# An encoder block with expert retrieval: three quarters of the expert input stage first, selection and gates spread and queued behind weight splits, output groups on two sets of PSUM banks

## The chip, the core and the metric

The kernel runs on one core of one Trainium2 chip. The metric is the device time of one execution in microseconds (us). The engines are PE (TensorE, matmuls), DVE (VectorE), ACT (ScalarE), POOL (GpSimd) and SP (SyncE, which here only issues DMAs). Each engine executes its own instruction stream in order.

## The reference

The block has 256 tokens of width 2048. Token mixers and a cross-attention come first; the change touches only the last part, the retrieval of single-neuron experts:

```python
def peer_ffn(a, w_pq, sub_keys, expert_u, expert_v):
    q = (t @ w_pq).reshape(T, PEER_HEADS, 2, PEER_HALF)
    s = jnp.einsum('thpd,pnd->thpn', q, sub_keys)
    top_s, top_i = lax.top_k(s, PEER_TOPK)                 # 16 of 128 keys, twice per head
    cand = top_s[:, :, 0, :, None] + top_s[:, :, 1, None, :]
    best_s, best_c = lax.top_k(cand.reshape(T, PEER_HEADS, 256), PEER_TOPK)
    i1 = take_along_axis(top_i[:, :, 0], best_c // 16); i2 = take_along_axis(top_i[:, :, 1], best_c % 16)
    expert = i1 * PEER_KEYS + i2                            # one of 16384
    gate = jax.nn.softmax(best_s, axis=-1)
    pre = jnp.einsum('bd,bed->be', t, expert_u[expert])
    act = jax.nn.gelu(pre, approximate=False) * gate
    return jnp.einsum('be,bed->bd', act, expert_v[expert])
```

## The kernel before

For 224 of the 256 tokens (T) the kernel computes all 16384 experts densely and lets a gate that is zero for the unchosen ones do the selecting. For the other 32 tokens it fetches only the chosen rows of `peer_u` and `peer_v` (the sparse part). All matrices are float32; a weight tile is split into a high part `wh` and a rest `wl`, which the PE multiplies one after the other.

**Weight tiles.** The dense part streams 256 tiles of 128x2048 floats (1 MB each). `wtile` (L89 to L101) loads one into a `w` buffer (three, issued by SP), lets ACT cast it to `wh` (L96) and DVE subtract `wl` (L98). With `pool=512` DVE takes 1536 columns and POOL the other 512 (both L101). There are two `wh` and two `wl` buffers. `last_split[0]` remembers the latest DVE split, and `tc.issue_after(last_split[0])` puts an instruction behind it in DVE's order.

**Input stage**, `u_steps(q)`, q = 0 to 3, 32 tiles each: 16 pairs of matmuls (L840 with `wh`, L841 with `wl`), then ACT copy, DVE add and ACT gelu into `P{j//16}` (L843 to L845). Each P tile holds 16 tiles' results, an eighth of the experts. There is not room for all eight, so P0 and P1 are written to DRAM (`pd`) and read back later. In the first quarter (q = 0) POOL helps with the split.

**Selection**, `key_steps` (the key scores' rest, `side`) and `select_steps(1)`, `select_steps(0)`: top 16 of the candidates, softmax, and one-hot products (L725, L731, L732) that look up the indices, all on DVE, 40 steps spread over the first 31 tiles. Nothing ties them to the splits.

**Gates**, `gate_steps`: 28 groups of 8 tokens. DVE makes one-hot matrices (L866 twice, L868 twice: a set), PE multiplies them (L883, 16 small matmuls), ACT copies the result (L893), and POOL writes it to DRAM (`gd`, L898). They are spread over 25 tiles of `u_steps(1)`.

**Preparation**, `prep_steps(c)`: loads the gates of P tile c in two halves (b = 0, 1; L923, by SP, each into one of the three `w` buffers), multiplies eight rows of P by each half (L919, eight DVE instructions), and splits the product into `a` (L107 on ACT, L108 on DVE).

**Output stage**, `v_steps(q)`, 32 tiles each, two chunks c per call in the order of the list `order` (n counts the chunks): per chunk four groups `ds` of four tiles (e = 0 to 3). A group accumulates 4 outputs (f) in four PSUM banks, all from the pool `acc` of four banks (L965 with `wh`, L969 with `wl`). DVE adds them to `yT` in two instructions for each f (L975, L976), and the next group's first matmul into a bank waits for its L976.

**Sparse part**, `sparse_steps`: 32 gathers of `peer_u` rows, each followed by one DVE product and sum (L794), and 32 of `peer_v`, each by a DVE multiply-add (L810). POOL issues each gather (L769) into one of three row buffers. It is spread over 174 tiles from the first preparation on. At its end it is folded in by matmuls (L821, L822).

The tiles are executed in this order: u0 (with selection), u1 (with gates), preparation of c = 2, v0, u2 (with the preparation of c = 4 in its last 7 tiles), v1, u3 (preparation of c = 6 in its last 7), v2, v3.

Of the kernel before, what the change touches and what calls it, by code (L numbers as in the profile page):

```python
# [9 lines left out]
F32 = mybir.dt.float32  # L10
# [4 lines left out]
ALU = mybir.AluOpType  # L15
AX = mybir.AxisListType

P = 128
# [9 lines left out]
TB = 8  # L28
SP = 32
T = S - SP  # L30
# [4 lines left out]
def block_kernel(ctx: ExitStack, tc: tile.TileContext, a: dict, out: bass.AP):  # L35
    nc = tc.nc

    const = ctx.enter_context(tc.tile_pool(name="const", bufs=1))
    stream = ctx.enter_context(tc.tile_pool(name="stream", bufs=2))
# [5 lines left out]
    dram = ctx.enter_context(tc.tile_pool(name="dram", bufs=1, space=bass.MemoryType.DRAM))  # L45
# [8 lines left out]
    def acc(name):  # L54
        return ps_acc.tile([P, 512], F32, tag="acc", name=name)
# [27 lines left out]
    n_w = [0]  # L83
    last_split = [None]

    def wtile(src, pool=0, parts=1):
        n_w[0] += 1
        w = stream.tile([P, D], F32, tag="w", name=f"w{n_w[0]}", bufs=3)
        nc.sync.dma_start(w, src)  # L89
        wh = stream.tile([P, D], F32R, tag="wh", name=f"wh{n_w[0]}")  # L90
        wl = stream.tile([P, D], F32R, tag="wl", name=f"wl{n_w[0]}")
        n = D // parts
        for i in range(parts):
            c = slice(i * n, (i + 1) * n)
            with tc.issue_after(after[-1]) if parts == 4 else nullcontext():
                nc.scalar.copy(wh[:, c], w[:, c])  # L96
            if not pool:
                last_split[0] = nc.vector.tensor_tensor(wl[:, c], w[:, c], wh[:, c].bitcast(F32), op=ALU.subtract).ins  # L98
        if pool:
            for e, c in ((nc.vector, slice(0, D - pool)), (nc.gpsimd, slice(D - pool, D))):  # L100
                i = e.tensor_tensor(wl[:, c], w[:, c], wh[:, c].bitcast(F32), op=ALU.subtract).ins  # L101
                if e is nc.vector:
                    last_split[0] = i
        return wh, wl
# [244 lines left out]
    side = ()  # L349
# [217 lines left out]
    side = ()  # L567
# [194 lines left out]
    act = small.tile([P, SP], F32, tag="act", name="act", bufs=1)  # L762
    hx = None

    bufs = []

    def rows_of(src, k):
        g = bufs[k % 3]
        nc.gpsimd.indirect_dma_start(  # L769
            g, None, src, bass.IndirectOffsetOnAxis(sx[:, 0, k : k + 1].bitcast(U32), 0)  # L770
        )
        return g

    def sparse_input():

        two = [X([P, 2, D], F32, f"rows{i}") for i in range(2)]
        bufs.extend((two[0][:, 1], two[1][:, 0], two[1][:, 1]))
        xs, gb = two[0][:, 0], bufs[2]
        rs = small.tile([P, 1], F32, tag="rs", name="rs", bufs=1)
        bcast_rows(gb, a["g_ffn"])  # L780
        for g in range(NG):
            p = slice(g * SP, (g + 1) * SP)
            nc.gpsimd.dma_start(xs[p], hd[T:S])
            nc.gpsimd.dma_start(rs[p], rf_[P - SP : P, 1:2])
        yield
        with tc.issue_after(last_split[0]):
            nc.vector.scalar_tensor_tensor(xs, xs, rs, gb, op0=ALU.mult, op1=ALU.mult)
        yield xs
# [33 lines left out]
            nc.vector.tensor_tensor(hx[:, 1, fs], hx[:, 1, fs], ps, op=ALU.add)  # L822
        yield

    pd = dram.tile([2, P, 16, T], F32, tag="pd", name="pd")


    ptiles = {}
# [1 line left out]
    def u_steps(q):  # L830

        for j in range(32 * q, 32 * q + 32):
            if j % 16 == 0:
                ptiles[j // 16] = X([P, 16, T], F32, f"P{j // 16}")
            po = acc(f"u{j}")
            wh, wl = wtile(a["peer_uT"][j], 512 if q == 0 else 0)
            wh = wh.rearrange("p (k i) -> p k i", k=NK)
            wl = wl.rearrange("p (k i) -> p k i", k=NK)
            for k in range(NK):
                nc.tensor.matmul(po[:, 0 : 2 * T], wh[:, k, :], aT.both(k), start=(k == 0), stop=False)  # L840
                nc.tensor.matmul(po[:, 0:T], wl[:, k, :], aT.tiles[k // 8][:, k % 8, 0], start=False, stop=(k == NK - 1))  # L841
            pre = ptiles[j // 16][:, j % 16, :]
            nc.scalar.copy(pre, po[:, T : 2 * T])  # L843
            nc.vector.tensor_tensor(pre, po[:, 0:T], pre, op=ALU.add)  # L844
            nc.scalar.activation(pre, pre, AF.Gelu)  # L845
            if j % 16 == 15 and j < 32:
                nc.gpsimd.dma_start(pd[j // 16], ptiles.pop(j // 16))
            yield

# [57 lines left out]
    def prep_steps(c):  # L907

        if c not in ptiles:
            ptiles[c] = X([P, 16, T], F32, f"P{c}b")  # L910
            nc.gpsimd.dma_start(ptiles[c], pd[c])
        pt = ptiles[c]
        g = []
        for b in range(3):
            if b > 0:
                with tc.issue_after(last_split[0]):
                    for j in range(8):
                        pv = pt[:, 8 * b - 8 + j, :].rearrange("p (b t) -> p b t", t=16)
                        nc.vector.tensor_tensor(pv, pv, g[b - 1][:, :, j, :], op=ALU.mult)  # L919
            if b < 2:  # L920
                n_w[0] += 1
                g.append(stream.tile([P, T // 16, 8, 16], F32, tag="w", name=f"w{n_w[0]}", bufs=3))
                nc.sync.dma_start(g[b], gd[:, 2 * c + b])  # L923
            yield
        for e in range(4):
            for i in range(2):
                ahl = M([P, 2, 2, T], F32R, f"a{c}_{e}{i}")
                j = 4 * e + 2 * i
                split(ahl[:, :, 0, :], ahl[:, :, 1, :], pt[:, j : j + 2, :])
                parts[c, 2 * e + i] = ahl  # L930
            yield
# [2 lines left out]
    yT = None  # L934
    gf = None

    order = [2, 3, 4, 5, 6, 7, 0, 1]

    def v_steps(q):

        nonlocal gf, hx, yT
        for n in range(2 * q, 2 * q + 2):
# [7 lines left out]
            if n == 7:  # L950
                gf = X([P, D], F32, "gf")
                bcast_rows(gf, a["g_final"])
            nxt = prep_steps(order[n + 1]) if n in (0, 2, 4, 5, 6) else iter(())
            for ds in range(4):
                po = [acc(f"v{c}_{ds}_{f}") for f in range(4)]
                for e in range(4):
                    wh, wl = wtile(a["peer_vP"][((2 * c + e // 2) * 4 + ds) * 2 + e % 2])
                    wh = wh.rearrange("p (j f) -> p j f", j=4)
# [35 lines left out]
    def run_spread(main, n_main, side, n_side):  # L994

        done = 0
        for i, _ in enumerate(main):
            due = n_side if i >= n_main - 1 else (i + 1) * n_side // n_main
            while done < due:
                next(side, None)  # L1000
                done += 1

    def with_last(main, n, side):

        for i, _ in enumerate(main):
            if i >= 32 - n:
                next(side, None)
            yield

    run_spread(u_steps(0), 31, chain(side, select_steps(1), select_steps(0)), 4 + 18 + 18)  # L1010
    sp = sparse_input()
    next(sp)
    run_spread(u_steps(1), 25, gate_steps(), T // TB + 1)
    xs = next(sp)
    rest = chain(
        prep_steps(2),
        v_steps(0),
        with_last(u_steps(2), 7, prep_steps(4)),
        v_steps(1),
        with_last(u_steps(3), 7, prep_steps(6)),  # L1020
        v_steps(2),
        v_steps(3),
    )
    run_spread(rest, 174, sparse_steps(xs), 2 * SP + 1)


    r = rstd_of(ssq_f, "final")
# [65 lines left out]
```

## Time and profile before

| | us |
|---|---|
| time, median of 3 runs (lowest, highest) | 2614.22 (2614.06, 2616.01) |
| the profiled execution: its own time | 2612.45 |
| the profiled execution: its span | 2610.7 |
| in it, PE busy | 2463.8 |
| in it, DVE busy | 1680.0 |
| in it, ACT busy | 1159.7 |

Busy times of matmuls include their modelled ends, so a busy PE can still be slower than at full clock. The granted clock of a stretch is its mean, 1.00 being 2.4 GHz. The two lists that matter for the dense part are a table of busy times by stretch (its first tile starts at 1096.46 us, its last ends at 2598.60) and the list of what PE waited for.

### The profile page before, as it was taken

The numbers are of one execution on the slowest core, as the hardware profiler recorded it, in microseconds if no ns is written. First come the engines' busy times: TensorE is split into PE (matmuls) and PEld (weight loads), VectorE is DVE, ScalarE is ACT, GpSimd is POOL, SyncE is SP. The second block draws the span as 40 slices with busy tenths as digits, with TensorE's granted clock in tenths as the row PEclk, the third lists the DMA queues.
The fourth block names the chain that finished last, engine by engine and source line by source line (L and its number), as shares of the span: only waits on it lengthen the run. The fifth ranks groups of instructions, "written<-read, shape, count | busy, mean of one in ns | idle before, by whom it ended". The sixth has DMA issues, their size and how long they took to land. (4 is left out here: it accounts for less than half of the span.)

```text
span 2610.7 us, 34575 instructions
## 1 busy us (share of the span) xinstructions
PE 2463.8 (94%) x14266; PEld 2214.9 (85%) x14266; DVE 1680.0 (64%) x2121; ACT 1159.7 (44%) x1346; POOL 236.7 (9%) x184
## 2 busy tenths in 40 slices
PE   8999999999999999977999988999899999898897
PEld 7888888888888888967988878999888998888897
DVE  5556544456555455897377777766777767677665
ACT  5444444545444445533455544345434455343343
POOL 0000000000000000123611101012000122000000
PEclk9999999999999999988999989999999999999999
DMA  6554555555544555434877777777777778876463
GB/s 250 188 193 175 178 193 193 214 189 175 187 171 164 176 201 186 169 122 149 283 254 241 234 266 284 284 281 289 269 281 274 264 290 311 319 286 243 173 221 132
DMA packets 84798, 584.40 MB, mean 224 GB/s; under 512 B 9793, under 2 KB 9857, under 8 KB 18721
## 3 DMA queue, kind: packets, MB, share of 16 engines
q1 hardware_dynamic: 67904, 480.28, 52.1%
q0 software_dynamic: 16592, 101.88, 10.8%
q8 instruction: 112, 1.84, 0.3%
q14 instruction: 46, 0.37, 0.0%
q10 hardware_dynamic: 144, 0.03, 0.0%
HBM read 559.58 MB, written 22.54 MB: 223 GB/s over the span
## 5 line engine op out<-in xcount | busy, mean ns | idle before, releaser
L98 DVE TENSOR_TENSOR wl<-w,wh 128x2048 fp32r<-128x2048 f32 (+2 forms) x432 | 936.6, 2172 | 759.4 <-ACT wh L96 759.0
L96 ACT CAST wh<-w 128x2048 fp32r<-128x2048 f32 (+2 forms) x464 | 841.8, 1819 | 875.1 <-PE v L965 308.4
L965 PE MATMUL v<-a,wh 128*128 128x448 f32 x2048 | 663.8, 383 | 47.3 <-DVE yT L976 40.7
L840 PE MATMUL u<-a,wh 128*128 128x448 f32 x2048 | 666.3, 383 | 4.8 <-ACT wh L96 4.8
L841 PE MATMUL u<-a,wl 128*128 128x224 f32 x2048 | 552.1, 270 | 39.9 <-DVE wl L101 32.7
L969 PE MATMUL v<-a,wl 128*128 128x224 f32 x2048 | 548.0, 268 | 10.4 <-DVE wl L98 10.4
L965 PEld LDWEIGHTS v<-a,wh 128*128 128x128 f32 x2048 | 392.5, 192 | 85.3 <-ACT wh L96 24.6
L841 PEld LDWEIGHTS u<-a,wl 128*128 128x128 f32 x2048 | 400.8, 196 | 44.9 <-DVE wl L101 36.0
L840 PEld LDWEIGHTS u<-a,wh 128*128 128x128 f32 x2048 | 394.0, 192 | 36.5 <-ACT wh L96 5.6
L969 PEld LDWEIGHTS v<-a,wl 128*128 128x128 f32 x2048 | 399.1, 195 | 12.6 <-DVE wl L98 11.8
L845 ACT ACTIVATE P<-P 128x224 f32<-128x224 f32 x128 | 50.1, 392 | 319.4 <-DVE P L844 319.3
L122 PE MATMUL g<-wh,x 128*128 128x512 f32 x256 | 100.2, 391 | 0.0
L124 PE MATMUL g<-wl,x 128*128 128x512 f32 x256 | 99.6, 389 | 0.0
L123 PE MATMUL g<-wh,x 128*128 128x512 f32 x256 | 99.6, 389 | 0.0
L101 DVE TENSOR_TENSOR wl<-w,wh 128x1536 fp32r<-128x1536 f32 x32 | 57.7, 1802 | 60.6 <-ACT wh L96 60.6
L101 POOL TENSOR_TENSOR wl<-w,wh 128x512 fp32r<-128x512 f32 x32 | 75.9, 2373 | 201.5 <-ACT wh L96 164.2
L144 PE MATMUL qk<-x,wh 128*128 128x512 f32 x256 | 91.8, 403 | 0.2 <-DVE qk L150 0.2
L144 PE MATMUL mq<-hq,wh 128*128 128x512 f32 x256 | 90.8, 398 | 0.0
L144 PE MATMUL pq<-hf,wh 128*128 128x512 f32 x256 | 90.8, 398 | 0.0
L769 POOL DMA_INDIRECT rows<-in_peer_v,sx x32 | 54.6, 1706 | 391.9 <-DVE rows L810 327.3
L144 PE MATMUL mk<-mem,wh 128*128 128x512 f32 x256 | 89.7, 394 | 0.0
L769 POOL DMA_INDIRECT rows<-in_peer_u,sx x32 | 51.6, 1613 | 374.4 <-DVE act L794 347.5
(322 smaller groups left out, 3474.4 us busy)
## 6 DMA issues: line engine op xcount, KB each, us to landing
w<-in_peer_uT SPq DMA_DIRECT2D x128, 1024.0 KB, 4.9
w<-in_peer_vP SPq DMA_DIRECT2D x128, 1024.0 KB, 4.9
w<-in_w_in SPq DMA_DIRECT2D x72, 1024.0 KB, 4.9
w<-in_mem_w_kv SPq DMA_DIRECT2D x32, 1024.0 KB, 4.8
w<-in_w_out SPq DMA_DIRECT2D x16, 1024.0 KB, 4.8
w<-in_mem_w_q SPq DMA_DIRECT2D x16, 1024.0 KB, 4.9
w<-in_mem_w_o SPq DMA_DIRECT2D x16, 1024.0 KB, 4.9
w<-in_peer_w_q SPq DMA_DIRECT2D x16, 1024.0 KB, 4.8
```

The source lines that it names most:

```text
L96: nc.scalar.copy(wh[:, c], w[:, c])
L98: last_split[0] = nc.vector.tensor_tensor(wl[:, c], w[:, c], wh[:, c].bitcast(F32), op=ALU.subtract).ins
L101: i = e.tensor_tensor(wl[:, c], w[:, c], wh[:, c].bitcast(F32), op=ALU.subtract).ins
L122: nc.tensor.matmul(po[b], xh, wh[:, k, :], start=(kk == 0), stop=False)
L123: nc.tensor.matmul(po[b], xl, wh[:, k, :], start=False, stop=False)
L124: nc.tensor.matmul(po[b], xh, wl[:, k, :], start=False, stop=(kk == nkc * 4 - 1))
L144: nc.tensor.matmul(po[f], wh[:, k, fs], xT.both(kk), start=(kk == 0), stop=False)
L769: nc.gpsimd.indirect_dma_start(g, None, src, bass.IndirectOffsetOnAxis(sx[:, 0, k : k + 1].bitcast(U32), 0))
L840: nc.tensor.matmul(po[:, 0 : 2 * T], wh[:, k, :], aT.both(k), start=(k == 0), stop=False)
L841: nc.tensor.matmul(po[:, 0:T], wl[:, k, :], aT.tiles[k // 8][:, k % 8, 0], start=False, stop=(k == NK - 1))
L965: nc.tensor.matmul(po[f][:, 0 : 2 * T], wh[:, j, fs], ahl.rearrange("p e t -> p (e t)"), start=first, stop=False,)
L969: nc.tensor.matmul(po[f][:, 0:T], wl[:, j, fs], ahl[:, 0, :], start=False, stop=last)
```

## The change

The order of the tiles becomes u0, u1, u2, v0, u3, v1, v2, v3. Everything beside the tiles becomes a track with a first tile, a last tile and a number of steps; the tracks wrapped in `paced` issue all their DVE work behind the latest split. Selection has tiles 0 to 46, gates 46 to 84, the sparse part 50 to 238. The second quarter too shares its splits with POOL. Four P tiles instead of two are written to DRAM and read back, and the list `order` begins with the four that stay. The gates of a preparation go, on POOL's queue, into a single buffer of their own, cut out of what was the third row buffer, so that two row buffers are left. In the output stage the groups with odd `ds` (but not in the last chunk) use the four banks of the pools `pst` and `psm`.

```diff
     def rows_of(src, k):
-        g = bufs[k % 3]
+        g = bufs[k % 2]
...
         two = [X([P, 2, D], F32, f"rows{i}") for i in range(2)]
-        bufs.extend((two[0][:, 1], two[1][:, 0], two[1][:, 1]))
-        xs, gb = two[0][:, 0], bufs[2]
+        bufs.extend((two[0][:, 1], two[1][:, 0]))
+        gates.append(two[1][:, 1, 0 : 8 * T].rearrange("p (b j t) -> p b j t", j=8, t=16))
+        xs, gb = two[0][:, 0], bufs[1]
...
-    pd = dram.tile([2, P, 16, T], F32, tag="pd", name="pd")
+    pd = dram.tile([4, P, 16, T], F32, tag="pd", name="pd")
...
-            wh, wl = wtile(a["peer_uT"][j], 512 if q == 0 else 0)
+            wh, wl = wtile(a["peer_uT"][j], 512 if q < 2 else 0)
...
-            if j % 16 == 15 and j < 32:
+            if j % 16 == 15 and j < 64:
                 nc.gpsimd.dma_start(pd[j // 16], ptiles.pop(j // 16))
...
-        g = []
+        g = gates[0]
...
-                        nc.vector.tensor_tensor(pv, pv, g[b - 1][:, :, j, :], op=ALU.mult)
+                        nc.vector.tensor_tensor(pv, pv, g[:, :, j, :], op=ALU.mult)
             if b < 2:
-                n_w[0] += 1
-                g.append(stream.tile([P, T // 16, 8, 16], F32, tag="w", name=f"w{n_w[0]}", bufs=3))
-                nc.sync.dma_start(g[b], gd[:, 2 * c + b])
+                nc.gpsimd.dma_start(g, gd[:, 2 * c + b])
...
-    order = [2, 3, 4, 5, 6, 7, 0, 1]
+    order = [4, 5, 6, 7, 0, 1, 2, 3]
...
-            nxt = prep_steps(order[n + 1]) if n in (0, 2, 4, 5, 6) else iter(())
+            nxt = prep_steps(order[n + 1]) if n in (0, 2, 3, 4, 5, 6) else iter(())
             for ds in range(4):
-                po = [acc(f"v{c}_{ds}_{f}") for f in range(4)]
+                kinds = (pst, pst, psm, psm) if ds % 2 and n < 7 else (acc,) * 4
+                po = [kind(f"v{c}_{ds}_{f}") for f, kind in enumerate(kinds)]
...
-    run_spread(u_steps(0), 31, chain(side, select_steps(1), select_steps(0)), 4 + 18 + 18)
...
-    run_spread(rest, 174, sparse_steps(xs), 2 * SP + 1)
+    def paced(steps):
+
+        while True:
+            with tc.issue_after(last_split[0]):
+                if next(steps, steps) is steps:
+                    return
+            yield
...
+    main = chain(u_steps(0), u_steps(1), u_steps(2), v_steps(0), u_steps(3), v_steps(1), v_steps(2), v_steps(3))
+
+    tracks = [
+        (paced(chain(side, select_steps(1), select_steps(0))), 0, 46, 4 + 18 + 18),
+        (input_steps(), 28, 46, 3),
+        (paced(gate_steps()), 46, 84, T // TB + 1),
+        (sparse_all(), 50, 238, 2 * SP + 1),
+        (prep_steps(order[0]), 88, 96, 7),
+        (prep_steps(order[2]), 152, 160, 7),
+    ]
+    done = [0] * len(tracks)
+    for i, _ in enumerate(main):
+        for n, (steps, lo, hi, of) in enumerate(tracks):
+            due = 0 if i < lo else min(of, (i + 1 - lo) * of // (hi - lo))
+            while done[n] < due:
+                next(steps, None)
+                done[n] += 1
```

The two kernels have the same matmuls in another order. Three places show what moves.

DVE in the selection, before: between the splits of two successive tiles (`wl193`, `wl194`) stands the add of the input stage (`P0`) and then sixteen instructions of the selection (`oh`, `sel`, `ex`, `cand`).

```order
L101 TENSOR_TENSOR wl193_8461<-w193_8458,wh193_8460 128x1536
L844 TENSOR_TENSOR P0_8017<-u6_8354,P0_8017 128x224
L732 TENSOR_REDUCE sel1_8248<-oh110_8753 128x32
L732 TENSOR_REDUCE sel1_8248<-oh111_8800 128x32
L725 TENSOR_TENSOR oh112_8848<-sel1_8248,iota_90 128x512
L725 TENSOR_TENSOR oh113_8896<-sel1_8248,iota_90 128x512
L731 TENSOR_TENSOR oh112_8848<-oh112_8848,top_7076 128x512
L731 TENSOR_TENSOR oh113_8896<-oh113_8896,top_7076 128x512
L732 TENSOR_REDUCE sel1_8248<-oh112_8848 128x32
L732 TENSOR_REDUCE sel1_8248<-oh113_8896 128x32
L737 SCALAR_TENSOR_TENSOR ex_8943<-sel1_8248 128x128
L689 TENSOR_TENSOR cand00_8960<-top_7076 128x512
```

DVE at the same kind of work in the changed kernel, some tiles later:

```order
L101 TENSOR_TENSOR wl201_8829<-w201_8826,wh201_8828 128x1536
L845 TENSOR_TENSOR P0_8017<-u14_8727,P0_8017 128x224
L725 TENSOR_TENSOR oh100_8868<-sel1_8334,iota_90 128x512
L731 TENSOR_TENSOR oh100_8868<-oh100_8868,top_7076 128x512
L732 TENSOR_REDUCE sel1_8334<-oh100_8868 128x32
L101 TENSOR_TENSOR wl202_8876<-w202_8873,wh202_8875 128x1536
L845 TENSOR_TENSOR P0_8017<-u15_8780,P0_8017 128x224
L725 TENSOR_TENSOR oh101_8915<-sel1_8334,iota_90 128x512
L731 TENSOR_TENSOR oh101_8915<-oh101_8915,top_7076 128x512
L732 TENSOR_REDUCE sel1_8334<-oh101_8915 128x32
L101 TENSOR_TENSOR wl203_8923<-w203_8920,wh203_8922 128x1536
```

The selection's instructions now stand three at a time between two splits.

POOL in the gates, before: after the spill of P1 it issues only the writes of gates, two for each pair of groups.

```order
L847 DMA pd_8014<-P1_8852 128x3584
L898 DMA gd_8015<-gs0_0_9764 128x8x128
L898 DMA gd_8015<-gs0_1_9765 128x8x128
L898 DMA gd_8015<-gs16_0_9908 128x8x128
L898 DMA gd_8015<-gs16_1_9909 128x8x128
```

POOL in the gates of the changed kernel (`rows0`, `rows1` are the sparse part's buffers):

```order
L899 DMA gd_8015<-gs0_0_10414 128x8x128
L899 DMA gd_8015<-gs0_1_10415 128x8x128
L101 TENSOR_TENSOR wl237_10637<-w237_10634,wh237_10636 128x512
L769 DMA rows0_9693<-in_peer_u,sx_8012 128x2048
L101 TENSOR_TENSOR wl238_10712<-w238_10709,wh238_10711 128x512
L101 TENSOR_TENSOR wl239_10785<-w239_10782,wh239_10784 128x512
L899 DMA gd_8015<-gs16_0_10603 128x8x128
L899 DMA gd_8015<-gs16_1_10604 128x8x128
L101 TENSOR_TENSOR wl240_10828<-w240_10825,wh240_10827 128x512
```

A quarter of each tile's split, and gathers, now stand between the writes.

DVE in the gates, before: two sets of one-hot instructions (`oe`, `o2`) stand between two splits, and none of the sparse part.

```order
L844 TENSOR_TENSOR P2_9673<-u47_10790,P2_9673 128x224
L866 TENSOR_TENSOR oe_136_10856<-iotax_92,i1T_7073 128x1024
L866 TENSOR_TENSOR oe_136_10856<-iotax_92,i2T_7074 128x1024
L868 TENSOR_TENSOR o2_136_10857<-oe_136_10856,gT_7075 128x1024 x2
L866 TENSOR_TENSOR oe_144_10929<-iotax_92,i1T_7073 128x1024
L866 TENSOR_TENSOR oe_144_10929<-iotax_92,i2T_7074 128x1024
L868 TENSOR_TENSOR o2_144_10930<-oe_144_10929,gT_7075 128x1024 x2
L98 TENSOR_TENSOR wl235_11011<-w235_11008,wh235_11010 128x2048
```

DVE in the gates of the changed kernel (L795 is L794 of before):

```order
L845 TENSOR_TENSOR P3_10370<-u59_11090,P3_10370 128x224
L867 TENSOR_TENSOR oe_72_11157<-iotax_92,i1T_7073 128x1024
L867 TENSOR_TENSOR oe_72_11157<-iotax_92,i2T_7074 128x1024
L795 ISA rows1_9694,act_8013<-rows1_9694,rows0_9693 128x2048
L795 ISA act_8013 128x1
L869 TENSOR_TENSOR o2_72_11158<-oe_72_11157,gT_7075 128x1024 x2
L867 TENSOR_TENSOR oe_80_11230<-iotax_92,i1T_7073 128x1024
L867 TENSOR_TENSOR oe_80_11230<-iotax_92,i2T_7074 128x1024
L869 TENSOR_TENSOR o2_80_11231<-oe_80_11230,gT_7075 128x1024 x2
L101 TENSOR_TENSOR wl247_11315<-w247_11312,wh247_11314 128x1536
```

A product of the sparse part has come in among the two sets.

## Rows read from the trace of the kernel before

**Rows 1.** Page part 1: busy time, share of the span, instructions of each engine.

```profile
PE 2463.8 (94%) x14266; PEld 2214.9 (85%) x14266; DVE 1680.0 (64%) x2121; ACT 1159.7 (44%) x1346; POOL 236.7 (9%) x184
```

**Rows 2.** Table by stretch: us, busy time (instructions) per engine, PE clock, DMA, GB/s.

```profile
1123.55:1216.84 93.29, 60.83 (x291) 54.72 (x289) 88.89 (x223) 27.96 (x34) 16.85 (x13) 0.82 0.29 103
...
1315.39:1489.01 173.62, 158.85 (x1250) 146.19 (x1249) 131.16 (x158) 95.02 (x188) 24.52 (x29) 0.99 0.76 247
...
1514.08:1538.07 23.99, 12.60 (x66) 11.19 (x65) 22.68 (x35) 9.19 (x15) 4.68 (x4) 0.72 0.90 335
1538.07:1704.50 166.43, 157.83 (x994) 148.28 (x993) 118.47 (x121) 67.77 (x57) 12.24 (x11) 1.00 0.78 279
...
1836.10:1875.82 39.72, 33.98 (x195) 31.24 (x193) 30.51 (x42) 19.49 (x27) 3.98 (x2) 0.91 0.76 272
1875.82:2054.39 178.57, 166.75 (x1026) 156.63 (x1025) 127.58 (x135) 65.77 (x45) 13.08 (x12) 0.97 0.76 272
2054.39:2184.81 130.42, 130.42 (x833) 124.49 (x833) 91.84 (x69) 65.21 (x76) 27.80 (x10) 1.00 0.76 281
2184.81:2220.82 36.01, 32.48 (x194) 30.12 (x193) 28.90 (x38) 19.23 (x27) 7.63 (x6) 0.95 0.94 356
2220.82:2510.05 289.23, 258.38 (x1547) 240.52 (x1545) 200.11 (x229) 104.57 (x75) 13.53 (x13) 0.95 0.70 253
...
sum 1502.14, PE 1377.45 PEld 1289.17 DVE 1066.84 ACT 646.41 POOL 212.63; mean PE 98.39 PEld 92.08 DVE 76.20 ACT 46.17 POOL 15.19
```

**Rows 3.** What PE waited for, 1090 to 2611: us in total, times, longest.

```profile
PE v L965 <- DVE yT L976: 40.7, 18, 6.2
PE u L841 <- DVE wl L101: 32.7, 11, 5.7
PE ps_g L883 <- DVE o L868: 14.7, 24, 2.7
```

**Rows 4.** Groups of instructions, 1315.39 to 1489.01: busy us, mean ns, idle before.

```profile
L98 DVE TENSOR_TENSOR wl<-w,wh 128x2048 fp32r<-128x2048 f32 x25 | 57.2, 2289 | 39.0 <-ACT wh L96 39.0
...
L868 DVE TENSOR_TENSOR o<-oe,gT 128x1024 f16<-128x1024 f16 x54 | 35.0, 689 | 1.0
...
L883 PE MATMUL ps_g<-o,oe 128*128 128x128 f16 x448 | 32.9, 219 | 14.8 <-DVE o L868 14.7
```

**Rows 5.** Groups of DVE, 1090 to 2611: the sparse products.

```profile
L794 DVE CUSTOM_DVE_ANT_0 rows<-rows,rows 128x2048 f32<-128x2048 f32 x21 | 48.0, 2283 | 0.0
```

**Rows 6.** Timelines in the selection (start us, us): POOL and DVE splits of two tiles.

```profile
1167.02 3.28 DVE L101 TENSOR_TENSOR wl<-w,wh 128x1536 fp32r<-128x1536 f32 x1
1167.40 1.27 POOL L101 TENSOR_TENSOR wl<-w,wh 128x512 fp32r<-128x512 f32 x1
...
1218.92 1.76 DVE L101 TENSOR_TENSOR wl<-w,wh 128x1536 fp32r<-128x1536 f32 x1 [4.03 <-ACT wh L96]
1218.97 2.86 POOL L101 TENSOR_TENSOR wl<-w,wh 128x512 fp32r<-128x512 f32 x1 [3.23 <-ACT wh L96]
```

**Rows 7.** Timelines at one end of an output group: DVE, then PE.

```profile
2388.91 0.38 DVE L975 TENSOR_TENSOR yT<-v,yT 128x224 f32<-128x224 f32 x1
2389.21 2.34 DVE L810 SCALAR_TENSOR_TENSOR rows<-rows,act,rows 128x2048 f32<-128x2048 f32 x1
...
2393.68 2.28 DVE L98 TENSOR_TENSOR wl<-w,wh 128x2048 fp32r<-128x2048 f32 x1
...
2392.00 0.71 PE L965 MATMUL v<-a,wh 128*128 128x448 f32 x1 [2.16 <-DVE yT L976]
```

**Rows 8.** Timelines around one gate load: SP, DVE, ACT.

```profile
2255.29 0.33 SPq L923 DMA_DIRECT2D w<-gd  x1
...
2260.20 2.50 DVE L919 TENSOR_TENSOR P<-P,w 128x224 f32<-128x224 f32 x8
...
2266.96 1.90 ACT L96 CAST wh<-w 128x2048 fp32r<-128x2048 f32 x1 [9.00 <-DMA w<-in_peer_vP]
```

**Rows 9.** DMA issues: count, median us to landing.

```profile
rows<-in_peer_u,sx POOLq DMA_INDIRECT x32, 6.1
```

More of the change, by code (lines that the diff above doesn't have):

```diff
@@ L763, in block_kernel @@
     hx = None
-    bufs = []
+    bufs, gates = [], []
     def rows_of(src, k):
-        g = bufs[k % 3]
+        g = bufs[k % 2]
         nc.gpsimd.indirect_dma_start(
@@ L1001, in run_spread, with sparse_all, input_steps @@
                 done += 1
[L1003 to L1007, printed above, removed]
-            yield
-    run_spread(u_steps(0), 31, chain(side, select_steps(1), select_steps(0)), 4 + 18 + 18)
[L1011 to L1023, printed above, removed]
-    run_spread(rest, 174, sparse_steps(xs), 2 * SP + 1)
+    def paced(steps):
[3 more added lines that the diff above has]
+                    return
+            yield
+    xs = []
+    def sparse_all():
+        yield from sparse_steps(xs[0])
+    def input_steps():
+        for x in sparse_input():
+            xs.append(x)
+            yield
+        xs.pop(0)
+    main = chain(u_steps(0), u_steps(1), u_steps(2), v_steps(0), u_steps(3), v_steps(1), v_steps(2), v_steps(3))
[14 more added lines that the diff above has]
+                done[n] += 1
     r = rstd_of(ssq_f, "final")
```

## The prediction

> **What bounds the kernel now.** I read the shares of the engines first: PE is busy for 94% of the span, DVE for 64% [rows 1]. So the PE is the bound, and only what lets it wait or slows its clock can be won. Which stretches those are, the table by stretch tells. An undisturbed stretch, the 26 plain tiles of u3, takes 130.42 us, or 5.016 us a tile, at clock 1.00 [rows 2]. The 256 tiles together take 1502.1 us [rows 2], while 256 times 5.016 is 1284.1: 218.0 us lie above the pace. By stretch, each as its time less its tiles at 5.016 [rows 2]: selection (9 tiles) 48.1; gates (25) 48.2; preparation of c = 2 (2) 14.0; the first output stretch (31) 10.9; u2's tail with a preparation (6) 9.6; the second output stretch (32) 18.1; u3's tail (6) 5.9; the third output stretch (48) 48.5. What is left of 218.0, some 14.7, lies in stretches of a few us each and in the last chunk.
>
> What the PE waits for there comes from the list of its waits [rows 3]: the adds into `yT` in the output stage (40.7 us in 18 waits), the splits with POOL in the selection (32.7 in 11), the one-hot matrices in the gates (14.7 in 24). All three are DVE. So DVE is idle a third of the time and late where its work stands in a lump.
>
> **Selection.** Before, up to sixteen small instructions stand between two splits; in that stretch DVE is busy for 88.89 of 93.29 us and the clock falls to 0.82 [rows 2]. The change removes no instruction; it puts the steps behind splits, 40 over 46 tiles. A tile then asks DVE for a split of 1.76 us [rows 6], an add of 0.4, and three one-hot instructions of some 0.7 each [the like of rows 4, 689 ns]: about 4.3 us of 5.016. That fits; one lump of small instructions at the join of the parts still makes a split late by some 2 us. I take 4 us for what remains of 48.1, with 2 and 12 as ends. Gain 44.
>
> **Gates.** They keep their work and get new neighbours. The 28 groups' matmuls are real PE work: 448 of them [rows 4], about 1.0 us a group where PE waits for nothing, so 28 us. The rest of the 48.2 is waiting and clock, 20. After the change, 38 tiles carry the 28 sets, which alone would thin out the waits; but the sparse part starts at tile 50 now, so that some 12 of its products (65 steps over 188 tiles, 34 tiles of them here) of 2.28 us [rows 5] fall into this stretch, some among two sets between two splits. Two sets are about 8 x 0.69 = 5.5 us; with a product 7.8, more than a tile's 5.016 plus its group. I count ten ordinary waits for one-hots of 1.0, three with a product inside of 3.1, two late splits of together 3.8, and 3 for clock: 26. To this comes POOL's quarter of the split, which this stretch did not have. In the selection a POOL split takes 1.27 us alone, but 2.86 when DVE's split began just ahead of it, and DVE's takes 3.28 instead of 1.76 when POOL's falls into it [rows 6]: one waits out the other. One-hot instructions and products read two inputs as the split does. I put 8 us on this: some 14 of the 38 tiles meet, with 0.6 on the path each, the rest covered by the tile of cushion in the two `wl` buffers. Sum 28 + 26 + 8 = 62. The ends: 48 (28, the 14.7 of [rows 3] and 5) and 75 (28, 14.7, all twelve products at 2.3, and 5). Loss 14. POOL's queue has the writes of gates and the gathers ahead of its splits now; the writes wait for ACT's copies of the gates, but the cast that the split needs stands behind those copies on ACT anyway, so I put nothing on it.
>
> What these rows show has a rule in the Trainium skill, "SBUF — State Buffer", section "Who interferes with whom": a DVE instruction with two SBUF inputs contends with a GpSimd instruction that reads SBUF, and the second to issue is blocked until the first ends. The trace agrees: 3.28 is 1.76 and rather more than the 1.27. The rule speaks against this edit. By it, with every one of the 38 POOL splits shutting DVE out for 1.27 us on the path, the stretch would cost 48 more instead of 8; this is the rival B below, worked out there from the rows.
>
> **Preparations.** The three that stand beside input tiles or alone cost 14.0 + 9.6 + 5.9 = 29.5. Two remain, each in the last eight tiles of an input quarter. Each has two lots of eight multiplies, 2.5 us [rows 8], splits of 0.6 each, and now a sparse instruction. With one gate buffer the second load starts only when the first multiplies are done and lands, by the like of a gather, 6.1 us later [rows 9], so that DVE can stand before it. I take 9.5 each, the dearer of the two tails, 19 together; ends 13 and 26. Gain 10.5.
>
> **Output stage.** Outside the last chunk it holds 10.9 + 18.1 + 48.5 = 77.5. Of this 40.7 are waits for `yT` [rows 3]. They go, as the next group's first matmuls get other banks. What is late next? At the end of a group a sparse multiply-add of 2.34 us slips between the adds, and the split behind them starts at 2393.68 instead of some 2391.4 [rows 7]. Before, the PE waited 2.16 us for the bank and this late split was hidden behind that wait, then the tile ran at a lower clock (0.71 us for a matmul in [rows 7]). After, the PE goes on at once: from 2389.8 one tile of 5.016 lasts to 2394.8, while the split ends at 2396.0. It waits 1.2 to 1.5 us instead of some 4 (an estimate: 2.16, and about a third of a tile lost at the lower clock). I count nine such, 13 us. Second, a gate load sat in one of three `w` slots until its multiplies were done, and the cast after it waited 9.00 us for its weights [rows 8]; with a buffer of its own this goes. What remains besides: the joins of input and output quarters and lots of multiplies, some 7; the fold of the sparse part, about 10, unchanged; two more spills and reads of P and the like, 6. Together 36; ends 22 and 60. Gain 41.
>
> **Two row buffers** instead of three: a gather is issued when the product before last is done, and has 2 x 2.9 tiles, some 14 us from one step to the next, against 6.1 for its landing [rows 9]. Nothing. The last chunk keeps its banks; with the 14.7 of the small stretches it stays.
>
> **Sum.** Selection 4, gates 62, preparations 19, output 36, rest 14.7: 135.7 for 218.0, a gain of 82. The profiled execution took 2612.45, so 2530; the median of the runs lies 1.8 above it: **2532 us**.
>
> **The rivals.** *A, the banks only change the name of the wait:* the splits are as late as the banks were. For it: the sparse instruction in [rows 7] delays both. Against: the split stands a tile ahead. Then 31 of the 40.7 stay: 2563. That the change doesn't do what it says would look like this.
> *B, POOL and DVE lock in the gates:* for it [rows 6]; against, the selection's plain tiles ran at the pace with POOL's 2.86. If each of 38 tiles pays 0.8 to 1.27 on the path, 30 to 48 instead of 8, the time is 2554 to 2572.
> *C, the stalls get so short that the clock holds:* the stretches with clock under 0.96 [rows 2] are those with stalls of several us. With every term at its lower end (2 + 48 + 13 + 22 + 14.7 = 99.7) the gain is 118: 2496.
> *D, slower than before:* the gathers, gate loads, spills and reads of P and writes of gates share POOL's queue, and with two row buffers one late transfer holds the next. The products stand in DVE's order between splits, so a late gather stops the splits behind it. Over 65 steps it takes 82 / 65 = 1.3 us each to eat the gain, that is, landings of about 15.5 us instead of 6.1 [rows 9]. At 2.0 us each it gives 2614 + 130 - 82 = 2662. Against it: 14 us of slack at every step.
>
> **How the numbers follow.** Forecast 0.62, C 0.14, A 0.12, B 0.08, D 0.04. The range leaves out half of C, D, and the upper edges of A and B: 2495 to 2574. A measurement of this kernel can tell about 0.2%, 5 us, from no change. All cases but D are faster by far more: 0.95, allowing a little for D at small size; within 0.2% 0.01; slower 0.04.
>
> **What would show it.** Right: in the selection no wait for a split over 3 us, and the clock near 1.00; no wait of L965 for `yT` outside the last chunk, and short ones (1 to 2 us) for `wl` in their place; no cast waiting 9 us for weights; the gates' 38 tiles at 239 to 266 us (190.6 for the tiles, and 48 to 75), with waits for one-hots. Wrong: waits for splits in the output stage adding up to over 30 us (A); POOL or DVE splits in the gates of 3 us at most tiles with PE behind them (B); DVE waiting for `rows` (D).

## The result, and the profile after

The changed kernel takes 2538.9 us (median of 4 runs, 2532.45 to 2540.6) where the kernel before takes 2614.14 (2611.39 to 2616.01): a ratio of 0.971, 95% interval 0.969 to 0.973. The forecast was 2532, its range 2495 to 2574. The profiled execution took 2540.41 us, its span is 2538.4.

Page part 1 of the changed kernel, to be read beside [rows 1]: PE is busy for 15.8 us less, DVE for 26 us and POOL for 74 us more.

```profile
PE 2448.0 (96%) x14266; PEld 2203.0 (87%) x14266; DVE 1706.1 (67%) x2121; ACT 1158.3 (46%) x1346; POOL 310.9 (12%) x236
```

The table by stretch of the changed kernel (us, busy time of PE, PEld, DVE, ACT, POOL with instructions, PE clock, DMA share, GB/s), to be read beside [rows 2]. The stretches are: selection (tiles 5 to 47), gates (48 to 84), u2's tail with the first preparation and the two tiles behind it (90 to 97), the rest of v0 (98 to 127), u3 (128 to 153), its tail and one tile (154 to 160), v1 to the fold (161 to 238), the fold (239, 240), the rest (241 to 255).

```profile
1125.84:1356.75 230.91, 222.60 (x1385) 209.36 (x1383) 199.06 (x329) 112.81 (x135) 103.86 (x56) 0.99 0.67 230
1356.75:1610.16 253.41, 225.39 (x1635) 209.10 (x1633) 193.85 (x207) 124.64 (x224) 84.93 (x57) 0.97 0.79 276
1635.22:1691.83 56.61, 47.52 (x259) 43.72 (x257) 36.14 (x46) 24.08 (x32) 4.28 (x5) 0.88 0.70 243
1691.83:1844.33 152.50, 151.03 (x963) 143.56 (x961) 113.20 (x117) 66.08 (x55) 12.49 (x12) 1.00 0.80 286
1844.33:1977.02 132.69, 130.89 (x834) 124.42 (x833) 88.30 (x75) 64.83 (x77) 18.54 (x9) 1.00 0.76 278
1977.02:2023.02 46.00, 39.42 (x227) 36.21 (x225) 33.81 (x41) 22.10 (x30) 7.99 (x8) 0.93 0.85 310
2023.02:2425.08 402.06, 394.19 (x2499) 373.36 (x2497) 329.08 (x372) 167.25 (x115) 39.83 (x37) 1.00 0.84 309
2425.08:2442.75 17.67, 15.33 (x74) 12.07 (x73) 11.96 (x18) 5.40 (x6) 0.00 (x0) 0.90 0.50 173
2442.75:2526.22 83.47, 80.91 (x514) 75.13 (x512) 50.78 (x59) 31.07 (x26) 0.00 (x0) 1.00 0.41 140
```

At 5.016 us a tile these stretches lie above the pace by 15.2, 67.8, 16.5, 2.0, 2.2, 10.9, 10.8, 7.6 and 8.2 us. The first five tiles add 1.9, tiles 85 to 89 nothing: all 256 tiles lie 143 us above the pace, for 218.0 before. 75 us have gone, all from this part of the program. (The execution that was profiled started its first tile 2.4 us later than the one before, so the two profiled executions differ by 72.)

What PE waited for, in the changed kernel from 1090 to 2540 (us, times, longest), beside [rows 3], and the longest of its waits for a split, from the timeline:

```profile
PE ps_g L884 <- DVE o L869: 22.5, 22, 2.9
PE u L842 <- DVE wl L98: 11.8, 9, 1.9
PE u L842 <- DVE wl L101: 10.5, 6, 3.2
PE v L969 <- DVE wl L98: 9.3, 12, 1.0
...
1134.42 0.37 PE L842 MATMUL u<-a,wl 128*128 128x224 f32 x1 [3.19 <-DVE wl L101]
```

The 40.7 us for `yT` are gone, the 32.7 for the selection's splits have become 10.5, and the one-hots have risen from 14.7 to 22.5. The longest wait for a split, 3.19 us, comes in tile 6, where the steps of the key scores meet those of the selection: there some 8 us of small DVE instructions still stand between two splits. In place of the banks stand twelve short waits for a split, 9.3 us. One of them, on DVE and PE, at a group end like that in [rows 7]:

```profile
2325.91 0.39 DVE L975 TENSOR_TENSOR yT<-v,yT 128x224 f32<-128x224 f32 x1
2326.21 2.35 DVE L811 SCALAR_TENSOR_TENSOR rows<-rows,act 128x2048 f32<-128x2048 f32 x1
...
2330.69 2.28 DVE L98 TENSOR_TENSOR wl<-w,wh 128x2048 fp32r<-128x2048 f32 x1
...
2333.03 0.37 PE L969 MATMUL v<-a,wl 128*128 128x224 f32 x1 [0.96 <-DVE wl L98]
2333.23 0.38 PE L965 MATMUL v<-a,wh 128*128 128x448 f32 x1
```

The sparse multiply-add still stands between the adds and the split is still late by its length, but PE waits 0.96 us instead of 2.16. Its next matmul of 448 columns takes 0.38 us, where the one in [rows 7] takes 0.71: the granted clock is 1.00 (2.4 GHz) from 2333 to 2338 us, and was 0.50 (1.2 GHz) from 2392 to 2394 before.

### The profile page after: what moved, and what is told of

The parts are those of the page before. It is cut to its first block, busy times and chain, and to the rows that moved or that the text cites. A ratio compares the mean times of both kernels' runs of the same rounds, so it can differ in the third digit from the quotient of the medians.

```text
span 2538.4 us, 34530 instructions
## 1 busy us (share of the span) xinstructions
PE 2448.0 (96%) x14266; PEld 2203.0 (87%) x14266; DVE 1706.1 (67%) x2121; ACT 1158.3 (46%) x1346; POOL 310.9 (12%) x236
## 5 line engine op out<-in xcount | busy, mean ns | idle before, releaser
L98 DVE TENSOR_TENSOR wl<-w,wh 128x2048 fp32r<-128x2048 f32 (+2 forms) x400 | 863.2, 2163 | 654.5 <-ACT wh L96 654.0
L965 PE MATMUL v<-a,wh 128*128 128x448 f32 x2048 | 648.9, 377 | 3.5 <-DVE P L845 3.5
L842 PE MATMUL u<-a,wl 128*128 128x224 f32 x2048 | 549.8, 269 | 22.5 <-DVE wl L98 11.8
L965 PEld LDWEIGHTS v<-a,wh 128*128 128x128 f32 x2048 | 386.0, 188 | 34.1 <-DVE P L845 4.0
L969 PEld LDWEIGHTS v<-a,wl 128*128 128x128 f32 x2048 | 392.5, 192 | 13.8 <-DVE wl L98 13.1
L101 POOL TENSOR_TENSOR wl<-w,wh 128x512 fp32r<-128x512 f32 x64 | 144.1, 2252 | 259.6 <-ACT wh L96 244.4
L101 DVE TENSOR_TENSOR wl<-w,wh 128x1536 fp32r<-128x1536 f32 x64 | 122.7, 1917 | 59.3 <-ACT wh L96 59.3
L769 POOL DMA_INDIRECT rows<-in_peer_v,sx x32 | 48.5, 1517 | 323.4 <-DVE rows L811 280.3
```

Source lines behind the costliest of these rows:

```text
L769: nc.gpsimd.indirect_dma_start(g, None, src, bass.IndirectOffsetOnAxis(sx[:, 0, k : k + 1].bitcast(U32), 0))
L965: nc.tensor.matmul(po[f][:, 0 : 2 * T], wh[:, j, fs], ahl.rearrange("p e t -> p (e t)"), start=first, stop=False,)
L969: nc.tensor.matmul(po[f][:, 0:T], wl[:, j, fs], ahl[:, 0, :], start=False, stop=last)
```

## The experiments

Each stands beside runs of the kernel before on the same chip. Every kernel but the second is the changed one with edits. The runs of the changed kernel alone spread over 8 us, so two of these kernels that lie 3 or 4 us apart are not told apart by their times.

**One set of banks.**

```diff
-                kinds = (pst, pst, psm, psm) if ds % 2 and n < 7 else (acc,) * 4
+                kinds = (acc,) * 4
```

> The changed kernel with all output groups in the four banks of acc again, all else as changed (2538.9 us). Theory (the banks were the wait, and the late splits behind a sparse instruction cost less than the banks did): the waits of L965 for yT come back, about 2.2 us each at 9 or more group ends, with a slow tile behind, and the short waits for wl (1 us, 9.3 us in all) go; 25 to 45 us more, 2564 to 2584. Rival A (the banks only change the name of the wait): 2531 to 2547.

Measured: 2566.5 us, ratio to before 0.981 (0.979 to 0.983); 28 us more than the changed kernel. The waits for `yT` are back, in 18 places:

```profile
PE v L965 <- DVE yT L976: 24.9, 18, 2.2
```

The time lies in the theory's range, and rival A falls. The 24.9 us are less than the 40.7 of [rows 3], though: the long ones, up to 6.2 us, are missing.

**The kernel before with two sets of banks.** The same line, put into the kernel before.

> The kernel before with one edit: odd output groups outside the last chunk in the banks of pst and psm. Theory: the 40.7 us of waits for yT go, with the clock behind them, and some 13 us of late splits come; the gate loads that hold a weight buffer stay; 25 to 50 us less than before, 2564 to 2589. Rival A: 2605 to 2614. If the waits for weights behind a gate load and the waits for yT are one stall counted twice, the gain is under 25.

Measured: 2594.1 us, ratio 0.992 (0.989 to 0.994); 20 us less, where 25 to 50 were expected. The first line is of the kernel before, the others show what came in place of the waits for `yT`:

```profile
PE v L969 <- DVE wl L98: 10.4, 4, 6.6
...
PE v L970 <- DVE wl L98: 25.5, 17, 6.6
...
PE v L966 <- ACT wh L96: 8.4, 5, 3.0
```

So some 23 of the 40.7 us turned into waits for splits and casts. In the kernel before, some waits that bore the banks' name had a second cause behind them, as the last sentence of the expectation allowed.

**Gate loads in the weight buffers.**

```diff
...
-        g = gates[0]
+        g = []
...
-                nc.gpsimd.dma_start(g, gd[:, 2 * c + b])
+                n_w[0] += 1
+                g.append(stream.tile([P, T // 16, 8, 16], F32, tag="w", name=f"w{n_w[0]}", bufs=3))
+                nc.sync.dma_start(g[b], gd[:, 2 * c + b])
```

> The changed kernel with the gate loads as they were: two loads on SP's queue into the weight buffers, and three row buffers. Theory (a gate load in a weight buffer delays the weights behind it): casts wait for weights again, 4 to 9 us each at most of the six preparations inside the output stage; 10 to 30 us more, 2549 to 2569, less some 4 us in the input tails, where the second load no longer waits for the first multiplies. Rival (the second set of banks hides that delay too): 2531 to 2543.

Measured: 2575.1 us, ratio 0.984 (0.982 to 0.987); 36 us more, above the range. Casts of ACT wait for weights 24 times; the second line is of the changed kernel:

```profile
ACT wh L96 <- DMA w<-in_peer_vP: 102.4, 24, 9.4
...
ACT wh L96 <- DMA w<-in_peer_vP: 9.7, 3, 4.2
```

The stretch from v1 to the fold goes from 10.8 to 52.8 us above the pace, while the two input tails get 9 us shorter. The gate loads are the dearer of the two delays of the output stage. The edit moves their buffer, their queue and the number of row buffers together; that it is the weight buffer is read from the casts' waits for weights, and no run parts the three.

**Neither edit of the output stage.** Both diffs above together.

> The changed kernel with both edits of the output stage undone: all output groups in the four banks of acc, and the gate loads in the weight buffers with three row buffers. Undoing the banks alone cost 28 us, undoing the gate loads alone 36. Theory (the two delays fall on the same group ends, and the PE pays the longer of the two): less than their sum, 2580 to 2594. Rival (they add up): 2598 to 2608.

Measured: 2601.5 us, ratio 0.995 (0.993 to 0.996); 62.6 us more than the changed kernel, where 28 and 36 add up to 64. My theory falls: the two add up. The list of waits, and ACT, DVE and PE at the place of PE's wait of 6.67 us:

```profile
PE v L966 <- DVE yT L977: 49.5, 20, 6.7
...
ACT wh L96 <- DMA w<-in_peer_vP: 80.3, 18, 9.5
...
2257.39 1.90 ACT L96 CAST wh<-w 128x2048 fp32r<-128x2048 f32 x1 [7.62 <-DMA w<-in_peer_vP]
...
2259.33 2.29 DVE L98 TENSOR_TENSOR wl<-w,wh 128x2048 fp32r<-128x2048 f32 x1 [4.81 <-ACT wh L96]
...
2264.63 0.71 PE L966 MATMUL v<-a,wh 128*128 128x448 f32 x1 [6.67 <-DVE yT L977]
```

The waits under the banks' name grow from 24.9 to 49.5 us when the gate loads hold weight buffers. A late cast makes a late split; DVE, in order, then comes late to the adds, and PE's wait is booked on `yT`. Why the banks alone gave 20 us in the kernel before and 26 here (2601.5 to 2575.1) was not pursued.

**The sparse part behind the gates.**

```diff
-        (sparse_all(), 50, 238, 2 * SP + 1),
+        (sparse_all(), 85, 238, 2 * SP + 1),
```

> The changed kernel with the sparse part spread over tiles 85 to 238 instead of 50 to 238, so that no product of it stands among one-hot sets. Theory (the products among the sets are the larger part of the new waits in the gates): the 36 gate tiles lose about 17 of the 67.8 us that they lie above 5.016 us a tile, and the output stage gains 3 to 6 us of late splits; 2522 to 2532. Rival B (POOL's split blocking one-hot instructions is the larger part): the gates lose under 5 us; 2536 to 2545.

Measured: 2517.5 us, ratio 0.963 (0.961 to 0.965); 21 us less than the changed kernel, below the range expected. The gates' stretch, 253.41 us there, is

```profile
1352.90:1581.05 228.15, 216.87 (x1634) 202.17 (x1633) 164.09 (x182) 123.81 (x223) 62.99 (x45) 1.00 0.72 249
```

25 us less, where 17 were expected; rival B falls. In the stretch PE's waits for one-hots go from 22.5 to 10.9 us, those for splits from 5.6 to 0.3, and the clock is back from 0.97 to 1.00, which is worth about 8 us of 253 (an estimate). The output stage pays some 9 of the 25 back, and the first input tail gives 6 more. What the product does among the sets is seen on DVE and POOL in the changed kernel; the last line is of another place:

```profile
1422.07 1.49 DVE L867 TENSOR_TENSOR oe<-iotax,i1T 128x1024 f16<-128x1024 f16 x1
...
1424.08 2.28 DVE L795 CUSTOM_DVE_ANT_0 rows<-rows 128x2048 f32<-128x2048 f32 x1
...
1427.50 2.25 DVE L867 TENSOR_TENSOR oe<-iotax,i1T 128x1024 f16<-128x1024 f16 x1
...
1431.60 1.75 DVE L101 TENSOR_TENSOR wl<-w,wh 128x1536 fp32r<-128x1536 f32 x1
...
1420.14 2.87 POOL L101 TENSOR_TENSOR wl<-w,wh 128x512 fp32r<-128x512 f32 x1 [1.44 <-ACT wh L96]
1426.64 1.23 POOL L769 DMA_INDIRECT rows<-in_peer_u,sx  x1 [3.63 <-DVE act L795]
1427.88 1.31 POOL L101 TENSOR_TENSOR wl<-w,wh 128x512 fp32r<-128x512 f32 x1
...
1484.82 0.69 DVE L867 TENSOR_TENSOR oe<-iotax,i1T 128x1024 f16<-128x1024 f16 x1 [5.71 <-DMA gd<-gs]
```

Some 9.5 us of DVE work (1422.07 to 1431.60) stand between two splits, 2.28 of it the product. Here the next gather waits for the product and stands ahead of POOL's split; so the split falls into the second set, and a one-hot instruction of 0.68 us takes 2.25. But the first one-hot, which no gather delayed, takes 1.49 beside POOL's split of its own tile. By the timelines of the whole stretch eleven one-hots are lengthened like this, four of them behind a gather; without the products there are still eleven. So most of the blocking stayed when the products left. A smaller part is POOL's queue: the last line shows DVE waiting for a write of gates that POOL issued behind a gather (PE waits 1.8 us there); in this run 0.6 is left of the 5.71.

**POOL in the first quarter only.**

```diff
-            wh, wl = wtile(a["peer_uT"][j], 512 if q < 2 else 0)
+            wh, wl = wtile(a["peer_uT"][j], 512 if q < 1 else 0)
```

> The changed kernel with POOL's share of the splits in the first input quarter only, as before; the gates' tiles have whole splits on DVE. Theory of the prediction (POOL's split and the one-hot instructions shut each other out, and that costs about 8 us net): the gates' tiles lose 4 to 15 us of their 67.8, 2524 to 2535. Rival (the 0.53 us that DVE saves at each split is worth more than the blocking costs): 2541 to 2555.

Measured: 2529.6 us, ratio 0.966 (0.963 to 0.969). The total agrees with the theory, and the rival falls. The gates' stretch carries 3.8 us of the 9 (249.65 for 253.41), just under the 4 to 15 expected. Tiles 32 to 47, which the edit also touches, give 1.4; the rest lies in stretches that it does not touch. The first line below is the stretch in this run. Then come the splits that DVE shares with POOL in the stretch of the changed kernel, and the first one-hot of each set: in the changed kernel, with the sparse part behind the gates, and here.

```profile
1353.52:1603.17 249.65, 225.13 (x1634) 209.20 (x1633) 188.44 (x207) 124.60 (x225) 51.30 (x42) 0.97 0.79 281
...
L101 DVE TENSOR_TENSOR wl<-w,wh 128x1536 fp32r<-128x1536 f32 x15 | 26.3, 1755 | 25.8 <-ACT wh L96 25.8
L867 DVE TENSOR_TENSOR oe<-iotax,i1T 128x1024 f16<-128x1024 f16 x27 | 30.1, 1116 | 5.7 <-DMA gd<-gs 5.7
...
L867 DVE TENSOR_TENSOR oe<-iotax,i1T 128x1024 f16<-128x1024 f16 x27 | 23.3, 861 | 0.6 <-DMA gd<-gs 0.6
...
L867 DVE TENSOR_TENSOR oe<-iotax,i1T 128x1024 f16<-128x1024 f16 x27 | 18.5, 684 | 5.6 <-DMA gd<-gs 5.6
```

All one-hots together keep DVE busy for 84.4, 81.6 and 71.9 us. Here no one-hot is lengthened, and yet the stretch lies 64.1 us above the pace at a clock of 0.97: the products cost without POOL's split too. As the line of L101 shows, only 15 of the 37 splits in the changed kernel's stretch are shared with POOL, since the second quarter ends with tile 63.

**No share on POOL at all.**

```diff
-            wh, wl = wtile(a["peer_uT"][j], 512 if q < 2 else 0)
+            wh, wl = wtile(a["peer_uT"][j], 0)
```

> The changed kernel with no share of the splits on POOL in any quarter: DVE makes every split whole (2.29 us instead of 1.76). Theory (with the selection and the gates in order behind the splits, DVE has the time, and POOL's split only blocks it): the gates' tiles gain 4 us as in the run with POOL in the first quarter only, and the selection's 15.1 us fall by 3 to 8; 2520 to 2530. Rival (the selection needs POOL's help: a tile asks DVE for about 4.8 of 5.016 us): 2533 to 2550.

Measured: 2535.9 us, ratio 0.970 (0.968 to 0.971): in the rival's range, at its low end, and not told apart from the changed kernel. The gates' stretch again falls, by 3.2 us, but the selection does not: 17.1 us above the pace for 15.2, and 3.2 for 1.9 ahead of it. Kernels with the selection unchanged lie between 14.1 and 18.0 there, so in the selection blocking and help cancel out as far as can be told.

**Selection not tied to the splits.**

```diff
-        (paced(chain(side, select_steps(1), select_steps(0))), 0, 46, 4 + 18 + 18),
+        (chain(side, select_steps(1), select_steps(0)), 0, 46, 4 + 18 + 18),
```

> The changed kernel with the selection spread over the same 46 tiles, but not tied to the splits. Theory (the order behind the splits removes the lumps, and the spread alone does not, since nothing holds the instructions back on DVE): tiles 5 to 48 lie 45 to 55 us above the pace as before, instead of 15.1; 30 to 40 us more, 2569 to 2579. Rival (the spread over more tiles is what helps): within 8 us, 2531 to 2547.

Measured: 2572.0 us, ratio 0.983 (0.981 to 0.986); 33 us more. The selection's tiles lie 51.5 us above the pace, and DVE's splits are late as in [rows 3]:

```profile
PE u L842 <- DVE wl L101: 35.2, 12, 5.6
```

**Selection in 31 tiles**, tied to the splits: the first line of that diff with 31 for 46.

> The changed kernel with the selection over 31 tiles instead of 46, still queued behind the splits. Theory (the order behind the splits is what helps): a tile asks DVE for at most some 4.5 us, under the pace of 5.016; within 6 us, 2533 to 2545. Rival (the spread is needed too): splits come late again, 10 to 30 us more.

Measured: 2538.1 us, ratio 0.969 (0.967 to 0.972), the same as the changed kernel. In the profiled execution, the slowest of the four, the selection lies 19.4 us above the pace for 15.2. The order behind the splits gives the gain here, and the spread none that the time shows.

**Preparations paced**, on top of the sparse part behind the gates.

```diff
-        (prep_steps(order[0]), 88, 96, 7),
-        (prep_steps(order[2]), 152, 160, 7),
+        (paced(prep_steps(order[0])), 85, 96, 7),
+        (paced(prep_steps(order[2])), 147, 160, 7),
```

The preparations inside `v_steps` are wrapped in `paced` too.

> The kernel with the sparse part over tiles 85 to 238 (2517.5 us) with one edit more: all instructions of the preparations are queued behind the splits, and the two preparations beside input tiles are spread over 11 and 13 tiles instead of 8. Theory (in these tails eight multiplies, four splits of the product and the casts that they need from ACT stand in one lump between two weight splits): the two tails, together 22.8 us above the pace, fall to 5 to 13; 2505 to 2513. Rival (the stall is the second gate load, which waits for the first multiplies): the lumps go but DVE waits as long for the load; 2514 to 2521.

Measured: 2516.0 us, ratio 0.961 (0.959 to 0.964): no change. That is the rival's time, but DVE waits for no gate load here. On DVE the products' splits left the lump, on ACT nothing moved:

```profile
1606.84 2.38 ACT L107 CAST a<-P 128x448 fp32r<-128x448 f32 x4 [2.42 <-DVE P L920]
1609.12 1.89 ACT L96 CAST wh<-w 128x2048 fp32r<-128x2048 f32 x1
```

Four casts wait for DVE's multiplies, and the weight cast waits behind them.

**Casts behind the weight casts**, on top of that.

```diff
+                last_cast[0] = nc.scalar.copy(wh[:, c], w[:, c]).ins
...
-                split(ahl[:, :, 0, :], ahl[:, :, 1, :], pt[:, j : j + 2, :])
+                with tc.issue_after(last_cast[0]):
+                    nc.scalar.copy(ahl[:, :, 0, :], pt[:, j : j + 2, :])
+                nc.vector.tensor_tensor(
+                    ahl[:, :, 1, :], pt[:, j : j + 2, :], ahl[:, :, 0, :].bitcast(F32), op=ALU.subtract
+                )
```

> The kernel with the preparations paced (2516.0 us) with one edit more: ACT's casts of the gated products stand behind the latest cast of a weight tile, two at a time, instead of four at once right behind the multiplies. Theory (ACT is what the tails wait for: four casts of 0.6 us that themselves wait for DVE's multiplies stand ahead of the next weight cast): the two tails lose 10 to 18 of their 23 us; 2497 to 2507. Rival (it is DVE's lump of product and multiplies alone): 2512 to 2520.

Measured: 2508.6 us, ratio 0.959 (0.957 to 0.960); 7.4 us less, just short of the theory. In the profiled executions the two tails, with all the tiles that the preparations now reach (85 to 97, 128 to 160), go from 23 to 16 us above the pace: ACT's order was about a third of their stall. Of what is left, the rival of the run before has a part: in the first tail DVE now waits for the second gate load,

```profile
1609.83 2.50 DVE L921 TENSOR_TENSOR P<-P,rows 128x224 f32<-128x224 f32 x8 [3.98 <-DMA rows<-gd]
```

a wait that is not there in the run before, where the casts were late.

**The last two together with POOL in the first quarter only.**

> The kernel with the casts behind the weight casts (2508.6 us) with POOL's share of the splits in the first quarter only. Theory (POOL's split only lengthens the waits for one-hots now that no product stands among them): eleven waits of 1.13 us become about 0.87, 3 us less, 2503 to 2508. Rival (the whole split, 0.53 us longer, makes splits late at the double sets): 2510 to 2518.

Measured: 2505.1 us (median of 5 runs, 2502.21 to 2507.66), ratio 0.958 (0.957 to 0.959), faster than the kernel before and, by 34 us, than the changed one. It is not told apart from the run before it (2508.6). The waits for one-hots total 9.6 us, where they were 10.8, and the gates' stretch is 2.2 us shorter:

```profile
1351.21:1577.04 225.83, 216.22 (x1634) 202.19 (x1633) 162.10 (x182) 124.02 (x224) 25.92 (x30) 1.00 0.73 252
```

This stretch has neither products nor POOL's splits. Beside the 249.65 us of the run with POOL in the first quarter only, it gives the price of the products, with their gathers, where POOL has no split: 24 us.

## Why the prediction was right, and where its terms were off

The bound (PE, kept waiting by DVE), the pace and the direction were read rightly, and the sum was off by 7 us: 135.7 us above the pace, measured 143. That closeness is partly luck, since three terms were off by more, in both directions (selection and preparations too low, the output stage too high), and two inside the gates hid each other.

*Selection.* Forecast 4 us (12 at most), and some 3 in the small stretches for the tiles behind; measured 15.2. The mechanism is shown: the order behind the splits does it (paced or not is 33 us). Two sizes were off. The lump at the join of the parts was put at some 2 us; it costs 5.1, a wait of 3.19 (the forecast's sign was none over 3) and a clock of 0.83 in that tile. And the term missed 8.0 us in tiles 34 to 40, where the sparse input is made: loads and gathers stand on POOL ahead of its splits, DVE's splits take up to 3.15 us, a DVE product of 2.34 stands ahead of a split, and one cast waits 3.05 for its weights. POOL's splits are the lesser part of it: in the run with POOL in the first quarter only, 6.6 of the 8.0 stay. What the others cost was not parted.

*Gates.* Forecast 62, measured 67.8, within the ends. Inside the sum two terms were off, in opposite directions. The products among the sets were put at about 13 us: three long waits, late splits and clock, most of the twelve costing nothing. Without them the stretch is 25 us shorter where POOL has splits and 24 where it has none, so each costs about 2 us with its gather, nearly its whole length of 2.28. POOL's split was put at 8, counted on 38 tiles. It reaches only to tile 63, which is 18 of them; taking it away gave 3.8 us with the products there and 2.2 without. So the two hardly depend on each other: the forecast's step that failed is how many products PE pays for. POOL's queue, put at nothing, made DVE wait 5.7 us once. Rival B's 30 to 48 us were not there, and with 18 such splits at 1.27 us they could not have come to more than 23. Its mechanism was there (2.25 us for 0.68). Rival A fell with the run with one set of banks.

*Preparations.* Forecast 19, 26 at most; measured 27.4 (16.5 and 10.9, with the tiles right behind). I named DVE's lump and the second load. Not named was ACT: its casts of the product stand ahead of the weight cast, and moving them gave 7 us.

*Output stage.* Forecast 36, 22 at least; measured 20.4 (2.0, 10.8, 7.6). The late split behind a sparse instruction was priced at 1.2 to 1.5 us, nine times; it is 1.0 at most, twelve times, and the clock stays at 1.00 there. The banks' own share was overrated, though: with one set only 24.9 of the 40.7 us of waits come back, and the time is 28 us longer. The larger share, 36, came from the gate loads, which the prediction removed without a price of its own. [rows 8] showed 9.00 us of such a wait at one place; the number of such places was not counted. So the stage gained 57 us where 41 were forecast.

*Two row buffers, POOL's queue (rival D).* DVE waited for no gather. The queue cost little: DVE waited 7.5 us in all for writes of gates and 4.3 for gate loads. *Rival C* (all terms at their lower ends) was not reached by the changed kernel; the clock did hold through the output stage.

## What to carry to other kernels

An engine that works in order delays what is behind it, so the useful question for each edit is which urgent instruction stands behind a long or waiting one, on every engine, and not only on the one that the list of waits names. Tie side work to the urgent stream's own instructions; spread over 46 tiles without a tie, the selection cost 51.5 us here, and 15.2 with it. Side work on an engine that the bottleneck waits for can cost nearly its whole length, although that engine is idle a quarter of the stretch: twelve products of 2.28 us, with their gathers, cost 24. And count the tiles that a term applies to in the code. Where two delays meet at one place, price each by the run without it, since the list of waits books both on the one that came last.

## What the runs showed of the hardware

Where DVE's instructions meet POOL's split, a one-hot of 0.68 us takes 1.48 to 2.57 in the changed kernel, and DVE's split of 1.76 takes 2.09 to 3.15. Each of these one-hots ends 0.55 us after POOL's split ended, each of these splits 1.6 us after it, whether DVE's record starts up to 1.9 us behind POOL's or up to 0.7 ahead of it. The Trainium skill, "SBUF — State Buffer", section "Who interferes with whom", has the second to issue blocked until the first ends. The trace agrees that one waits for the other's end; which was issued first the starts of the records do not tell. In the run with the casts behind the weight casts, a gate load that POOL issued at 1601.33 let DVE go only at 1609.83, 8.5 us later; the median landing of such loads was 5.0 us in that run, and 4.5 on SP's queue in the kernel before.
